# Squares, sums and a reciprocal rearranged for the last two row blocks of a fused matmul and RMS norm

## The chip, the cores and the metric

The kernel runs on one core of a Trainium2 chip. The metric is the time of one execution on the device in microseconds (us); the time before is the median of three runs. One further execution was profiled: the profile's span goes from its first instruction to its last, and its own time is a little longer.

Engine names: PE is the matrix engine (TensorE), DVE is VectorE, ACT is ScalarE, POOL is GpSimd, SP is SyncE, which here only issues transfers. Each engine works through its own queue in order, so an instruction that waits holds up everything queued behind it on that engine.

## The reference

```python
def setup_inputs():
    m, k, n = 2048, 2048, 2048
    # a: m x k, b: k x n, gamma: n, all float32; eps = 1e-5

def reference(a, b, gamma, eps):
    x = np.matmul(a, b)
    rms = np.sqrt(np.mean(x ** 2, axis=-1, keepdims=True) + eps)
    return (gamma * x / rms).astype(np.float32)
```

A row of the output can be scaled only when all 2048 elements of that row of the product are known, since the root takes the mean over the whole row.

## The kernel before

The product's 2048 rows are 16 row blocks of 128, and its 2048 columns are four chunks of 512. A chunk of a row block, 128x512 in fp32, fills one bank of the accumulator memory (PSUM). The first four row blocks are worked as plain products. After that the kernel works on groups: group g holds row blocks 2g and 2g+1, and half j of a group holds two chunks of columns, so that a half is a 2x2 block of chunks. Each half is made by a scheme of seven products in place of eight (Strassen's, in Winograd's form): products 1 to 7 multiply quarters of A or sums of them by quarters of B or differences of them, and sums of the results give the four chunks x11 and x12 (upper row block, first and second chunk) and x21 and x22 (lower row block). `do(n, m)` issues product m of half n: eight matmuls at line 367 that add up into one bank, with the copies between banks that the scheme needs (lines 635 to 641). Some products are worked by the same scheme once more for two halves or groups together (`step` at line 406, `step_seven` at line 448).

The change lies in `last_group` (lines 859 to 985), the last group: g is 7, its row blocks are ra = 14 and rb = 15, and its halves are n and n+1. The code keeps the chunks of both halves in pairs, so x11[0] and x12[0] are row block 14's chunks 0 and 1, x11[1] and x12[1] its chunks 2 and 3, and x21 and x22 are the same for row block 15. TensorE's order at the end is product 6 of half n+1, products 5 of both halves, products 3 of both, products 4 of both. The chunks get complete as follows:

- x11[0] and x11[1] are complete before the last products; they lie in row block 14's output tiles, `xa` (columns 0 to 1023) and `x_tile(ra, 1)`.
- b3[0] and b3[1] are the banks that hold x22's products first. `nc.scalar.copy` at lines 935 and 940 takes them out when products 5 are done, and the sum with x21 gives x22[0] and x22[1], row block 15's chunks 1 and 3. Products 3 are then added on into the same banks, which makes them row block 14's chunks 1 and 3 (x12).
- b2[0] and b2[1] become row block 15's chunks 0 and 2 with products 4, the last of all.

For each row block the squares are made on ScalarE by `square_of` (line 275): one activation that squares its source, writes the squares to a scratch tile and leaves the sum over the row in a column of `msq`. Column 0 of `msq` holds the term with eps. `root` (line 293, the activation at 295) takes the square root of the last sum plus a bias `part`, which VectorE has added up from the earlier columns; `inverse` (line 298, instruction at 300) is VectorE's reciprocal.

What sets the order here is the order of the calls: the schedule is written by hand (`tc.manual_schedule()`), each engine gets its instructions in the order in which the code issues them, and the waits between engines follow from what they read and write. Two engines that read the same bank are also put in order.

After row block 14's reciprocal r_a, its four chunks are scaled by three engines: `by_r` (line 873, ScalarE) scales `left`, `by_r_pool` (line 876, GpSimd) scales `mid` and x11[1], all three already multiplied by gamma, and `scaled_gamma` (line 869, VectorE) multiplies b3[1] by both at once. SyncE's queue issues the transfers to the output in the order of the code (lines 960, 962 and 965). Row block 15 follows in the same manner (lines 971 to 985); its chunks 1 and 3, multiplied by gamma, stand in `wide`, and lines 982 and 985 issue its two transfers.

Of the kernel before, what the change touches and what calls it, by code (L numbers as in the profile page):

```python
# [8 lines left out]
FP32 = mybir.dt.float32  # L9
# [4 lines left out]
ALU = mybir.AluOpType  # L14
# [3 lines left out]
def kernel(  # L18
# [13 lines left out]
    nc = tc.nc  # L32
    P = 128
# [6 lines left out]
    CH = 512  # L40
# [62 lines left out]
    def add(out, in0, in1, op=ALU.add):  # L103
        nc.vector.tensor_tensor(out=out, in0=in0, in1=in1, op=op)  # L104
# [107 lines left out]
    msq = {}  # L212
# [62 lines left out]
    def square_of(mb, src):  # L275
        c = n_sq[mb]
        n_sq[mb] += 1
        sq = sq_pool.tile([P, 2 * CH], BF16, name="sq")
        nc.scalar.activation(out=sq[:, 0:src.shape[-1]], in_=src, func=ACTF.Square,  # L279
                             scale=inv_sqrt_n, accum_out=msq[mb][:, c:c + 1])  # L280

    def square_half(mb, h):
        square_of(mb, x_tile(mb, h))
# [9 lines left out]
    def root(last, part):  # L293
        rms = stat_pool.tile([P, 1], FP32, name="rms")
        nc.scalar.activation(out=rms, in_=last, func=ACTF.Sqrt, bias=part, scale=1.0)
        return rms
# [16 lines left out]
    def finish(mb, order=(0, 1)):  # L313
        if mb not in inverse_of:
            inverse_of[mb] = inverse(rms_of.pop(mb))
        for h in order:
            x = x_half.pop((mb, h))
            nc.vector.scalar_tensor_tensor(  # L318
                out=x, in0=x, scalar=inverse_of[mb], in1=gamma_sb[:, h * HALF:(h + 1) * HALF],
                op0=ALU.mult, op1=ALU.mult)  # L320
            nc.sync.dma_start(out=rows(mb, h * HALF, (h + 1) * HALF), in_=x)
# [302 lines left out]
    def do(n, m, copies=True):  # L624

        if n >= len(halves) or n < 0:
            return
        g, j = halves[n]
        b1, b2, b3 = B1[n % 2], B2[n % 2], B3[n % 2]
        if g >= G2:  # L630
            b1 = b2
        product(g, j, m, {1: b1, 2: b1, 3: b3, 4: b2, 5: b3, 6: b2, 7: B7}[m],
                start=m in (1, 7))
        if m == 1 and g >= G2:
            nc.scalar.copy(out=chunks(n)[0], in_=b2)
        elif m == 1:
            nc.scalar.copy(out=b2, in_=b1)
        elif m == 6:
            nc.scalar.copy(out=b3, in_=b2)  # L639
        elif m == 7 and copies:  # L640
            nc.scalar.copy(out=chunks(n)[2], in_=B7)

    def take(n, what, engine="A"):

        x11, x12, x21, x22 = chunks(n)
        if what == 11:
            copy_on(engine)(out=x11, in_=B1[n % 2])
        elif what == 12:
            copy_on(engine)(out=x12, in_=B3[n % 2])
        elif what == 22:  # L650
            add(x22, B3[n % 2], x21)
        else:
            add(x21, B2[n % 2], x21)
# [205 lines left out]
    def last_group():  # L859
        n = len(halves) - 2  # L860
        g = NG - 1
        ra, rb = 2 * g, 2 * g + 1
        x11, x12, x21, x22 = zip(chunks(n), chunks(n + 1))
        xa, xb = x_tile(ra, 0), x_tile(rb, 0)
        gam = [gamma_sb[:, c * CH:(c + 1) * CH] for c in range(NCH)]
        gam_left = gamma_sb[:, 0:HALF]

        def scaled_gamma(x, src, r, gamma_of_x):
            nc.vector.scalar_tensor_tensor(out=x, in0=src, scalar=r, in1=gamma_of_x,
                                           op0=ALU.mult, op1=ALU.mult)  # L870

        def by_r(x, r):
            nc.scalar.activation(out=x, in_=x, func=ACTF.Copy, scale=r)  # L873

        def by_r_pool(x, r):
            nc.gpsimd.tensor_scalar(out=x, in0=x, scalar1=r, scalar2=1.0,  # L876
                                    op0=ALU.mult, op1=ALU.mult)

        b2, b3 = [B2[(n + j) % 2] for j in range(2)], [B3[(n + j) % 2] for j in range(2)]
        x00, x01 = first_sums(n)[0:2]  # L880
        before = [chunks(n - 2), chunks(n - 1)]


        step_seven(1, B7)
        nc.scalar.copy(out=W2, in_=B7)
        do(n, 6)
        step_seven(6, B7)
        nc.scalar.copy(out=Y2, in_=B7)
        step_seven(2, W2)
        for c in (2, 3):  # L890
            add(before[0][c], W2, before[0][c])
        step_seven(5, Y2)
        nc.scalar.copy(out=x21[1], in_=Y2)
        step_seven(7, X2)
        nc.scalar.copy(out=x21[0], in_=X2)
        square_half(rb - 2, 0)
        add(x21[1], X2, x21[1])
        step_seven(3, Y2)
        for c in (2, 3):
            add(before[1][c], Y2, before[1][c])  # L900
        take_pre(rb - 2)
        square_right(rb - 2)
        do(n - 1, 3)
        take(n - 1, 12)
        step_seven(4, B7)
        add(x21[0], B7, x21[0])
        add(b2[0], b2[0], x21[0])
        finish(rb - 2)


        step(g - 1, 1, X2)
        nc.scalar.copy(out=W2, in_=X2)
        do(n + 1, 1)
        step(g - 1, 6, X2)
        nc.scalar.copy(out=Y2, in_=X2)
        step(g - 1, 2, W2)
        add(x00, W2, x00)
        step(g - 1, 5, Y2)
        add(x11[1], Y2, x11[1])
        square_half(ra - 2, 0)  # L920
        step(g - 1, 7, B7)
        add(x11[0], B7, x11[0])
        add(x11[1], B7, x11[1])
        step(g - 1, 3, Y2)
        add(x01, Y2, x01)
        take_pre(ra - 2)
        square_right(ra - 2)
        step(g - 1, 4, X2)
        add(x11[0], X2, x11[0])
        a_sums(g, (4,))  # L930
        do(n + 1, 6)
        add(b2[1], b2[1], x21[1])
        finish(ra - 2)
        do(n, 5)
        nc.scalar.copy(out=x22[0], in_=b3[0])
        square_of(ra, x11[1])
        add(x22[0], x21[0], x22[0])
        add(x11[1], x11[1], gam[2], ALU.mult)
        do(n + 1, 5)
        nc.scalar.copy(out=x22[1], in_=b3[1])  # L940
        square_of(rb, x22[0])
        wide = a_pool.tile([P, K], FP32, name="a32")
        chunk = [wide[:, c * CH:(c + 1) * CH] for c in range(NCH)]
        add(chunk[1], x22[0], gam[1], ALU.mult)
        add(x22[1], x21[1], x22[1])
        do(n, 3)
        take(n, 12)
        square_half(ra, 0)
        pre_a = stat_pool.tile([P, 1], FP32, name="pre")
        nc.vector.tensor_scalar(out=pre_a, in0=msq[ra][:, 0:1], scalar1=msq[ra][:, 1:2],  # L950
                                scalar2=msq[ra][:, 2:3], op0=ALU.add, op1=ALU.add)
        add(xa, xa, gam_left, ALU.mult)
        do(n + 1, 3)
        square_of(ra, b3[1])
        rms_a = root(msq[ra][:, 3:4], pre_a)
        add(chunk[3], x22[1], gam[3], ALU.mult)
        r_a = inverse(rms_a)
        left, mid = xa[:, 0:CH], xa[:, CH:]
        by_r(left, r_a)
        nc.sync.dma_start(out=rows(ra, 0, CH), in_=left)  # L960
        by_r_pool(mid, r_a)
        nc.sync.dma_start(out=rows(ra, CH, HALF), in_=mid)
        by_r_pool(x11[1], r_a)
        scaled_gamma(x12[1], b3[1], r_a, gam[3])
        nc.sync.dma_start(out=rows(ra, HALF, N), in_=x_tile(ra, 1))
        square_of(rb, x22[1])
        pre_b = stat_pool.tile([P, 1], FP32, name="part")
        nc.vector.tensor_scalar(out=pre_b, in0=msq[rb][:, 0:1], scalar1=msq[rb][:, 1:2],
                                scalar2=msq[rb][:, 2:3], op0=ALU.add, op1=ALU.add)
        do(n, 4)  # L970
        square_of(rb, b2[0])
        add(xb[:, 0:CH], b2[0], gam[0], ALU.mult)
        part = stat_pool.tile([P, 1], FP32, name="part")
        add(part, pre_b, msq[rb][:, 3:4])
        do(n + 1, 4)
        last_sq = stat_pool.tile([P, 1], FP32, name="last_sq")
        sq = sq_pool.tile([P, 2 * CH], BF16, name="sq")
        nc.scalar.activation(out=sq[:, 0:CH], in_=b2[1], func=ACTF.Square, scale=inv_sqrt_n,
                             accum_out=last_sq)
        r_b = inverse(root(last_sq, part))  # L980
        nc.vector.tensor_scalar_mul(out=xb[:, 0:CH], in0=xb[:, 0:CH], scalar1=r_b)
        nc.sync.dma_start(out=rows(rb, 0, CH), in_=xb[:, 0:CH])
        by_r(wide.rearrange("p (c n) -> p c n", n=CH)[:, 1::2, :], r_b)
        scaled_gamma(chunk[2], b2[1], r_b, gam[2])
        nc.sync.dma_start(out=rows(rb, CH, N), in_=wide[:, CH:])
# [40 lines left out]
```

## Time and profile before

| | us |
|---|---|
| median of 3 runs | 219.46 (219.31 to 219.65) |
| the profiled execution's own time | 219.09 |
| its span | 217.3 |
| PE busy in the span | 207.2 (95%) |
| DVE busy | 168.9 (78%) |
| ACT busy | 114.8 (53%) |
| POOL busy | 35.6 (16%) |
| last transfer issued (start of the issue, from the span's start) | 212.88 |

The busy share is a mean over the whole span, so it tells nothing of the last ten microseconds, where the matrix engine runs out of work before the others do. For those the timeline is read: one line for each instruction with its start, its duration, the engine, the line of the code, the operation, and what it writes and reads by the names of the tiles. Row block 14's output tiles appear there as `x`, row block 15's as `x` (columns 0 to 1023) and, before they are copied to the tile named `a`, in a reused buffer named `t_left`; banks appear as `acc`. An instruction with an accumulator output has a second line, the reading of the accumulator.

### The profile page before, as it was taken

How to read it: one execution, taken by the hardware profiler on the slowest of the kernel's cores; microseconds unless marked ns; L12 is line 12 of the kernel's file. 1: busy time of each engine (PE TensorE's matmuls, PEld its weight loads, DVE VectorE, ACT ScalarE, POOL GpSimd, SP SyncE). 2: the span in 40 equal slices, each digit the busy share in tenths (PEclk: the TensorE clock that was granted, in tenths of full speed). 3: DMA queues.
4: the chain of work that ended last, by engine and by line, in shares of the span. 5: the costliest groups of instructions: out<-in, count | busy, mean ns of one | idle time of the engine just before them, and what ended most of it. 6: DMA issues, size and time to landing. Idle time of an engine off the chain costs nothing.

```text
span 217.3 us, 2979 instructions
## 1 busy us (share of the span) xinstructions
PE 207.2 (95%) x1016; PEld 96.2 (44%) x1016; DVE 168.9 (78%) x333; ACT 114.8 (53%) x225; POOL 35.6 (16%) x74
## 2 busy tenths in 40 slices
PE   7999999999999999999999999999999999999950
PEld 3444544444455444444444444444444444444420
DVE  1128869999899987888975899399759899688871
ACT  2110002900599569598626952594776834654761
POOL 7554444334001000100021001102010000000020
PEclk9999999999999999999999999999999999999996
DMA  7999999999959688988675975599996872040446
GB/s 155 173 202 210 200 206 208 213 208 216 403 192 383 285 233 234 302 354 244 157 239 176 337 244 91 193 238 265 263 317 161 267 133 82 14 186 10 193 134 252
DMA packets 37039, 46.60 MB, mean 214 GB/s; under 512 B 22560, under 2 KB 26656, under 8 KB 35744
## 3 DMA queue, kind: packets, MB, share of 16 engines
q0 software_dynamic: 10608, 23.86, 45.0%
q1 hardware_dynamic: 26144, 22.29, 34.1%
q10 hardware_dynamic: 272, 0.26, 0.3%
q8 instruction: 8, 0.13, 0.2%
q14 instruction: 7, 0.06, 0.1%
HBM read 34.60 MB, written 16.78 MB: 236 GB/s over the span
## 4 chain that ended last, share of the span: by engine, by line
PE 87%; DVE 4%; DMA 3%; ACT 2%; issue 1%; POOL 1%; ACTq 0%; POOLq 0%
PE acc L367 58%; PE acc L457 16%; DMA early<-in_a_dram 3%; PE acc L406 3%; PE acc L448 2%; PE tbank L406 2%; PE tbank L486 2%; PE tbank L188 2%; ACT sq L279 1%; DVE x L318 1%; DVE x L104 1%; ACT a L873 1%; POOL b L118 0%; PE acc L201 0%; PE tbank L201 0%
## 5 line engine op out<-in xcount | busy, mean ns | idle before, releaser
L457 PE MATMUL acc<-b,head_at 128*128 128x512 bf16 x176 | 43.0, 379 | 0.3 <-DMA b<-in_b_dram 0.3
L367 PEld LDWEIGHTS <-s 128*128 128x128 f16 (+1 forms) x280 | 27.4, 98 | 33.1 <-DVE s L344 0.3
L279 ACT ACTIVATE sq<-x 128x1024 bf16<-128x1024 f32 (+1 forms) x31 | 31.9, 1030 | 18.9 <-DVE x L104 14.3
L318 DVE SCALAR_TENSOR_TENSOR x<-x,r,gamma_sb 128x1024 f32<-128x1024 f32 x28 | 35.0, 1282 | 0.5
L367 PE MATMUL acc<-b,head_at 128*128 128x512 bf16 x136 | 33.8, 379 | 0.0
L104 DVE TENSOR_TENSOR x<-acc,x 128x512 f32<-128x512 f32 x34 | 22.7, 687 | 9.8 <-PE acc L406 4.2
L367 PEld LDWEIGHTS <-head_at 128*128 128x128 f16 (+1 forms) x192 | 18.7, 98 | 22.2
L367 PE MATMUL acc<-b,at_even 128*128 128x512 bf16 x112 | 26.1, 379 | 0.0
L457 PEld LDWEIGHTS <-head_at 128*128 128x128 bf16 x176 | 16.9, 98 | 19.6 <-issue 0.6
L230 ACT ACTIVATE sq<-a 128x1024 bf16<-128x1024 f32 x22 | 23.3, 1058 | 2.2 <-DMA a<-in_a_dram 1.7
L367 PE MATMUL acc<-b,s 128*128 128x512 bf16 x104 | 24.4, 379 | 0.0
L367 PEld LDWEIGHTS <-at_even 128*128 128x128 f16 x160 | 15.6, 98 | 18.6
L367 PE MATMUL acc<-early,s 128*128 128x512 bf16 x96 | 23.7, 379 | 0.0
L118 POOL DMA_DIRECT2D b<-in_b_dram x32 | 17.2, 540 | 20.5 <-DMA b<-in_b_dram 14.1
L367 PE MATMUL acc<-t_left,s 128*128 128x512 bf16 x80 | 18.9, 379 | 0.0
L496 ACT COPY x<-acc 128x512 f32<-128x512 f32 x7 | 4.0, 581 | 25.3 <-PE acc L457 25.3
L193 DVE COPY head_at<-tbank 128x1024 bf16<-128x1024 bf16 x7 | 4.8, 692 | 7.7 <-PE tbank L188 7.7
L639 ACT COPY acc<-acc 128x512 f32<-128x512 f32 x12 | 6.9, 574 | 7.4 <-PE acc L367 7.3
L104 DVE TENSOR_TENSOR x<-tbank,x 128x512 f32<-128x512 f32 x9 | 6.2, 691 | 4.2 <-PE tbank L486 4.1
L876 POOL TENSOR_SCALAR x<-x,r 128x512 f32<-128x512 f32 x2 | 1.4, 685 | 48.8 <-DVE r L300 48.8
L149 POOL CAST pace<-at_even 128x1 f32<-128x1 f16 x3 | 1.7, 551 | 37.5 <-DMA at_even<-a 37.5
L367 PE MATMUL acc<-early,head_at 128*128 128x512 bf16 x32 | 7.7, 379 | 0.0
(155 smaller groups left out, 259.6 us busy)
## 6 DMA issues: line engine op xcount, KB each, us to landing
out_dram<-x SPq DMA_DIRECT2D x29, 512.0 KB, 3.0
a<-in_a_dram POOLq DMA_DIRECT2D x9, 1024.0 KB, 6.3
b<-in_b_dram POOLq DMA_DIRECT2D x32, 256.0 KB, 9.9
a<-in_a_dram POOLq DMA_DIRECT2D x4, 512.0 KB, 9.8
early<-in_a_dram POOLq DMA_DIRECT2D x7, 256.0 KB, 10.0
gamma_sb<-in_gamma_dram POOLq DMA_DIRECT2D x2, 512.0 KB, 9.9
head_at<-in_a_dram POOLq DMA_DIRECT2D x1, 1024.0 KB, 9.4
out_dram<-x SPq DMA_DIRECT2D x3, 256.0 KB, 2.6
```

Source lines behind the costliest of these rows:

```text
L104: nc.vector.tensor_tensor(out=out, in0=in0, in1=in1, op=op)
L118: nc.gpsimd.dma_start(out=raw[j][kp][:, t, :], in_=b[lo:lo + P, j * HALF:(j + 1) * HALF])
L188: nc.tensor.matmul(view[:, t, r, :], ah(kp)[:, r, t * P:(t + 1) * P], identity, is_transpose=True, start=(t == 0 and r == 0), stop=(t == 1 ...
L193: nc.vector.tensor_copy(out=head_at[:, 2 * kp:2 * kp + 2, :, :], in_=view)
L230: nc.scalar.activation(out=junk, in_=a32[mb][:, h * HALF:(h + 1) * HALF], func=ACTF.Square, scale=2.0 ** -8, accum_out=n2[:, h:h + 1])
L279: nc.scalar.activation(out=sq[:, 0:src.shape[-1]], in_=src, func=ACTF.Square, scale=inv_sqrt_n, accum_out=msq[mb][:, c:c + 1])
L318: nc.vector.scalar_tensor_tensor(out=x, in0=x, scalar=inverse_of[mb], in1=gamma_sb[:, h * HALF:(h + 1) * HALF], op0=ALU.mult, op1=ALU.mult)
L367: nc.tensor.matmul(bank, lhsT[:, kp, :], rhs, start=(start and kp == 0), stop=(kp == KP - 1), skip_group_check=not start)
L406: nc.tensor.matmul(bank, lhsT[:, k, :], rhs, start=(m in (1, 7) and k == 0), stop=(k == KQ - 1), skip_group_check=m not in (1, 7))
L448: nc.tensor.matmul(bank, lhsT[:, k, :], rhs[:, k, :], start=(m in (1, 7) and k == 0), stop=(k == KQ - 1), skip_group_check=m not in (1, 7))
L457: nc.tensor.matmul(bank, head_at[:, kt, r, :], head_rhs(c, kt), start=(kt == 0), stop=(kt == KT - 1))
L639: nc.scalar.copy(out=b3, in_=b2)
```

## The change

Only the order and the grouping of the work in `last_group` change. Row block 14's chunk x11[0] is squared by itself ahead of line 935's copy. Its chunk 1 is no longer copied out of b3[0] into `xa` and squared there together with chunk 0 in one 1024-wide activation; it is squared out of the bank, and the multiply with gamma reads the bank and writes `mid`, while `left` is multiplied by itself. Row block 14 now has four sums of squares beside column 0 of `msq`, and the bias of its root is added up in two steps, `pre` and `pre_a`. The sum x22[1] moves ahead of the products 3, and its square moves from behind row block 14's scaling to the place behind b3[0]'s square, with the sum `pre_b` ahead of row block 14's reciprocal. The multiplies of x11[1] and of x22[0] with gamma move behind the two multiplies of row block 14's left half, and the multiply of x22[1] with gamma (`chunk[3]`) moves from the place ahead of the reciprocal `r_a` to the place behind row block 14's scaling.

TensorE's, GpSimd's and SyncE's instructions and their order stay the same. VectorE has two instructions more.

```diff
         add(b2[1], b2[1], x21[1])
+        square_of(ra, x11[0])
         finish(ra - 2)
         do(n, 5)
         nc.scalar.copy(out=x22[0], in_=b3[0])
         square_of(ra, x11[1])
         add(x22[0], x21[0], x22[0])
-        add(x11[1], x11[1], gam[2], ALU.mult)
         do(n + 1, 5)
         nc.scalar.copy(out=x22[1], in_=b3[1])
         square_of(rb, x22[0])
+        add(x22[1], x21[1], x22[1])
+        pre = stat_pool.tile([P, 1], FP32, name="pre")
+        nc.vector.tensor_scalar(out=pre, in0=msq[ra][:, 0:1], scalar1=msq[ra][:, 1:2],
+                                scalar2=msq[ra][:, 2:3], op0=ALU.add, op1=ALU.add)
+        do(n, 3)
+        square_of(ra, b3[0])
+        square_of(rb, x22[1])
+        left, mid = xa[:, 0:CH], xa[:, CH:]
+        add(mid, b3[0], gam[1], ALU.mult)
+        add(left, left, gam[0], ALU.mult)
+        add(x11[1], x11[1], gam[2], ALU.mult)
+        pre_a = stat_pool.tile([P, 1], FP32, name="pre")
+        add(pre_a, pre, msq[ra][:, 3:4])
+        do(n + 1, 3)
+        square_of(ra, b3[1])
+        rms_a = root(msq[ra][:, 4:5], pre_a)
         wide = a_pool.tile([P, K], FP32, name="a32")
         chunk = [wide[:, c * CH:(c + 1) * CH] for c in range(NCH)]
         add(chunk[1], x22[0], gam[1], ALU.mult)
-        add(x22[1], x21[1], x22[1])
-        do(n, 3)
-        take(n, 12)
-        square_half(ra, 0)
-        pre_a = stat_pool.tile([P, 1], FP32, name="pre")
-        nc.vector.tensor_scalar(out=pre_a, in0=msq[ra][:, 0:1], scalar1=msq[ra][:, 1:2],
-                                scalar2=msq[ra][:, 2:3], op0=ALU.add, op1=ALU.add)
-        add(xa, xa, gam_left, ALU.mult)
-        do(n + 1, 3)
-        square_of(ra, b3[1])
-        rms_a = root(msq[ra][:, 3:4], pre_a)
-        add(chunk[3], x22[1], gam[3], ALU.mult)
+        pre_b = stat_pool.tile([P, 1], FP32, name="part")
+        nc.vector.tensor_scalar(out=pre_b, in0=msq[rb][:, 0:1], scalar1=msq[rb][:, 1:2],
+                                scalar2=msq[rb][:, 2:3], op0=ALU.add, op1=ALU.add)
         r_a = inverse(rms_a)
-        left, mid = xa[:, 0:CH], xa[:, CH:]
         by_r(left, r_a)
         nc.sync.dma_start(out=rows(ra, 0, CH), in_=left)
         by_r_pool(mid, r_a)
         nc.sync.dma_start(out=rows(ra, CH, HALF), in_=mid)
         by_r_pool(x11[1], r_a)
         scaled_gamma(x12[1], b3[1], r_a, gam[3])
         nc.sync.dma_start(out=rows(ra, HALF, N), in_=x_tile(ra, 1))
-        square_of(rb, x22[1])
-        pre_b = stat_pool.tile([P, 1], FP32, name="part")
-        nc.vector.tensor_scalar(out=pre_b, in0=msq[rb][:, 0:1], scalar1=msq[rb][:, 1:2],
-                                scalar2=msq[rb][:, 2:3], op0=ALU.add, op1=ALU.add)
+        add(chunk[3], x22[1], gam[3], ALU.mult)
         do(n, 4)
```

## The prediction

> **What bounds the kernel now.** I read the page's chain first.
>
> ```profile
> PE 87%; DVE 4%; DMA 3%; ACT 2%; issue 1%; POOL 1%; ACTq 0%; POOLq 0%
> ```
>
> TensorE sets the end nearly everywhere, but the diff leaves TensorE's instructions and their order as they are, so the change can only act where TensorE no longer decides: the end. Next the timeline of the last 14 us, all engines (start, duration, engine, line, operation, and in brackets the idle time before it).
>
> ```profile
> 204.29 0.57 ACT L649 COPY x<-acc 128x512 f32<-128x512 f32 x1
> 205.79 1.89 PE L367 MATMUL acc<-t_left,head_at 128*128 128x512 bf16 x8
> 206.79 0.29 ACT L295 ACTIVATE rms<-msq,pre 128x1 f32<-128x1 f32 x1
> 207.40 0.68 DVE L104 TENSOR_TENSOR a<-t_left,gamma_sb 128x512 f32<-128x512 f32 x1
> 207.52 1.89 PE L367 MATMUL acc<-early,head_at 128*128 128x512 bf16 x8
> 208.00 0.16 DVE L300 RECIPROCAL r<-rms 128x1 f32<-128x1 f32 x1
> 208.19 0.72 ACT L873 ACTIVATE x<-x,r 128x512 f32<-128x512 f32 x1 [1.10 <-DVE r L300]
> 208.26 1.36 POOL L876 TENSOR_SCALAR x<-x,r 128x512 f32<-128x512 f32 x2 [48.84 <-DVE r L300]
> 208.82 0.61 ACT L279 ACTIVATE sq<-t_left 128x512 bf16<-128x512 f32 x1
> 209.55 0.60 ACT L279 ACTIVATE sq<-acc 128x512 bf16<-128x512 f32 x1
> 209.85 0.39 SPq L965 DMA_DIRECT2D out_dram<-x  x1
> 210.27 0.60 ACT L978 ACTIVATE sq<-acc 128x512 bf16<-128x512 f32 x1
> 210.28 0.69 DVE L104 TENSOR_TENSOR x<-acc,gamma_sb 128x512 f32<-128x512 f32 x1 [0.44 <-ACT sq L279]
> 211.13 0.29 ACT L295 ACTIVATE rms<-last_sq,part 128x1 f32<-128x1 f32 x1 [0.17 <-DVE part L104]
> 212.88 0.33 SPq L985 DMA_DIRECT2D out_dram<-a  x1
> ```
>
> Row 14's root was ready at 207.08 (206.79 + 0.29), yet its reciprocal ran at 208.00, behind the product of 207.40 on VectorE. TensorE's last product ended at 209.41 (207.52 + 1.89), yet its square (L978) began at 210.27: ScalarE was still scaling row 14 and squaring two other chunks, one of them from t_left (x22[1]), which had long been there. So 0.86 us of row 15's chain is ScalarE's queue. Then the transfers, in stretches of 0.25 us; the last two numbers are the DMA engines' busy share and GB/s.
>
> ```profile
> 212.25:212.50 0.25, 0.00 (x0) 0.00 (x0) 0.25 (x1) 0.25 (x1) 0.00 (x0) 1.00 1.00 410
> 212.50:212.75 0.25, 0.00 (x0) 0.00 (x0) 0.25 (x1) 0.25 (x1) 0.00 (x0) 1.00 0.53 213
> 212.75:213.00 0.25, 0.00 (x0) 0.00 (x0) 0.05 (x1) 0.10 (x1) 0.00 (x0) 1.00 0.10 33
> 213.00:213.25 0.25, 0.00 (x0) 0.00 (x0) 0.00 (x0) 0.00 (x0) 0.00 (x0) 1.00 0.90 344
> ```
>
> From 209.75 to 215.7 the DMA engines are busy with the two rows (2.1 MB at about 400 GB/s where undisturbed); only here, between row 14's last bytes and row 15's first, do they idle. Against 400 GB/s that is 0.12 + 0.23 + 0.04 = 0.38 us. So the end has two limits close together: row 15's arithmetic and the queue of bytes.
>
> **The parts, with their costs.** *Square of x11[0] added ahead of L935's copy (ScalarE).* It costs 0.63 us plus its accumulator read, 0.73 in all (from 203.66 to 204.39 for such a square of SBUF). ScalarE idles 1.16 us there, from 199.66 to 200.81, so it ends near 200.41: nothing. Without that cover L935's copy would move by up to 0.73, and TensorE, which adds to that bank from 202.34 while the copy ends at 201.40, would still not wait.
>
> *L649's copy replaced by a square out of PSUM, the 1024-wide square dropped, x22[1]'s square put here.* The square of b3[0] starts at 204.42 (after the accumulator read that ends at 204.39), is done with its read 0.69 later at 205.11; x22[1]'s follows to 205.87. The next one, of b3[1], can start when TensorE is done at 205.96; before it started at 206.07. Gain under 0.1, and not used (below). x22[1]'s sum, moved ahead on VectorE to 203.48, finds L940's copy done at 203.13: no wait, and its place is counted next.
>
> *VectorE up to the reciprocal.* Its adds of 128x512 start 0.61 apart (203.48, 204.09, 204.69). The product `mid` reads the bank that ScalarE squares and waits for it: by the row of 210.28, which started 0.04 behind such a square's read, at 205.15. Queued behind it: left, x11[1], pre_a, chunk[1], pre_b, the reciprocal; the root waits for pre_a. Their starts: 205.15 + 0.60 + 0.61 + 0.61 = 206.97 pre_a; + 0.07 (as between 197.30 and 197.37) chunk[1]; + 0.61 pre_b; + 0.19 (206.07 to 206.26) the reciprocal, at 207.84. The root, with pre_a at 207.12, ends near 207.5, so it doesn't decide. The reciprocal thus gains 0.16, not the 0.9 that its move suggests: the split product, the two new sums and the wait for the bank fill the place of the product moved behind it. Bounds: if the wait cost nothing it would come 0.6 earlier (bound by the root, at about 207.5, 0.5 of gain); if the new small sums each drained the engine for their whole length, about 0.25 later. I take 0.16.
>
> *Row 15's chain.* Scaling row 14 starts at 208.03; the square of b2[0] now follows at once, 208.66 to 209.35 with its read; the last square starts at TensorE's end, 209.44 (0.83 gained), its sum ready at 210.13. VectorE: L869's multiply at 208.03, chunk[3] 0.67 later at 208.70, b2[0]'s product behind the square of that bank at 209.39, part at 209.99 to 210.14, root 0.10 later at 210.24 against 211.13. So 0.89 is gained up to the root, and with it the issues of both last transfers (212.17 and 212.88), if nothing stands in chunk[3]'s way.
>
> *Something does: GpSimd.* chunk[3] reads two SBUF tiles while GpSimd scales x11[1]; before, VectorE idled there. The trace shows such meetings where GpSimd copies 128x1:
>
> ```profile
> 109.88 0.71 POOL L149 CAST pace<-at_even 128x1 f32<-128x1 f16 x1 [20.86 <-DMA at_even<-a]
> 158.34 0.18 POOL L149 CAST pace<-at_even 128x1 f32<-128x1 f16 x1 [7.96 <-DMA at_even<-a]
> 109.85 0.69 DVE L344 TENSOR_TENSOR at_even<-at_even 128x1024 f16<-128x1024 f16 x1
> ```
>
> With VectorE idle it took 0.18, beside a two-tile VectorE instruction 0.71, until that ended. Bounds: nothing; or VectorE waits for one GpSimd instruction, 0.68 (half of 1.36); or GpSimd waits for one VectorE instruction, 0.65. I take the last, since it is what the casts show: GpSimd's first scaling ends at 208.78 (208.26 - 0.16 + 0.68), chunk[3], waiting since 208.70, runs to 209.4, and GpSimd's second scaling from there to 210.1 (209.62 before), so that row 14's last issue (209.85) comes at 210.3. The Trainium skill (SBUF — State Buffer, section "SBUF: two separate sides") says that one port pair is shared, that a VectorE instruction with two SBUF inputs and a GpSimd one that reads SBUF exclude each other, and that the first holds it for the whole instruction; the casts agree (0.71 against 0.18). By it the first to start decides, so the sum would be mine or the rival's in which GpSimd goes first.
>
> *The bytes.* From issue to first bytes takes about 0.8 (208.94 to 209.75, 212.17 to 213.0). Row 14's first 512 KB flow from 209.6 to about 210.95; its last 512 KB, issued at 210.3, are ready at 211.1, as late as before when they stood behind the others. So row 14 ends where it did. Row 15's first bytes are ready at 212.1 and its others at 212.8, before row 14 is out: the idle 0.38 is filled, and the 0.89 of the chain is cut to that. Not all engines end together; I take 0.30 of it, bounds 0.1 to 0.38. **Sum:** the profiled execution, 219.09 (span 217.3 and 1.8 around it), becomes 218.79; the median of the runs is 0.37 above it, so 219.46 becomes 219.16.
>
> **Rivals.** *No meeting:* chunk[3] and GpSimd don't hold one another. Row 14 is then out 0.16 earlier and the gap filled as well: 0.46, 219.00. For it: GpSimd's first scaling ran at 0.68 beside a VectorE multiply, though that one read PSUM. Against: the casts.
>
> *GpSimd goes first:* chunk[3] waits to 209.46, b2[0]'s product starts at 210.07, the root at 210.92, 0.2 earlier than before; the bytes follow: 0.2, 219.26. For it: GpSimd's two scalings stood without a gap between them (1.36 for both). Against: in the casts it was GpSimd that waited.
>
> *The bytes aren't the limit:* row 14's transfers ran slower (287 and 262 GB/s in two of the stretches from 211.25 to 211.75), and if row 15's issue alone decides, up to 0.89 is gained: 218.57. Against: the volume and 400 GB/s.
>
> *Slower:* transfers that overlap disturb each other. When the third transfer came up behind two others near 210.7, the next four stretches gave 311, 426, 287 and 262 GB/s, mean 322. After the change row 15's transfers come up behind row 14's from 212.1 on, with 1.27 MB to go (225 KB of row 14 by the stretches from 212.1, and 1.05 MB). At 322 GB/s that takes 3.95 us and ends at 216.05 instead of 215.7: 0.35 slower, 219.81. It decides below 1.27 MB / 3.6 us = 353 GB/s. Against: two full-width transfers behind one another kept 408 GB/s between 203 and 205.
>
> **Chances.** Forecast 0.40, no meeting 0.20, GpSimd first 0.13, bytes not the limit 0.12, slower 0.15. A change under 0.2% (0.44 us) is what a measurement of this kernel can hardly tell from none: faster means under 219.02, slower over 219.90. Faster: all of the bytes rival (0.12), somewhat over half of the no-meeting one, which lies on the bound (0.12), and the part of the forecast in which the wait for the bank costs less than taken (0.12): 0.36. Slower by that much: a good half of the slow rival, whose rate may fall further: 0.09. Within: 0.55. The forecast's own range is 218.90 (the reciprocal earlier by half of its bound) to 219.36 (a gap filled by 0.1 alone). The range reaches from the near end of the bytes rival to the near part of the slow one: 218.68 to 219.65.
>
> **What would show it.** In the changed profile the reciprocal of row 14 stands near 207.84 and its neighbours on VectorE without idle time behind 205.15; the last square starts behind TensorE, near 209.44; chunk[3] or GpSimd's second scaling is longer than 0.69; the last root stands near 210.2; the DMA engines show no gap near 212.75 and end about 0.3 earlier. It is wrong if TensorE's last product starts later than 207.52, if the reciprocal is no earlier than 208.00, or if the bytes still pause and the time falls by the whole 0.89.

## The result

| | before | changed |
|---|---|---|
| median of 22 runs each, us | 219.39 | 218.89 |
| the profiled execution's own time, us | 219.09 | 218.90 |
| its span, us | 217.3 | 217.1 |

The ratio is 0.9974 with a 95% interval of 0.9963 to 0.9985: the change makes the kernel 0.15% to 0.37% faster, 0.50 us by the medians (0.30 was forecast; the 219.46 that the forecast started from was the median of the first three of these 22 runs). 218.89 is inside the predicted range, 0.27 below the forecast's 219.16. By the medians the gain is a little past the bound of 0.2%, so the case that had the chance of 0.36 came true and not the one of 0.55; the interval reaches to both sides of that bound.

Here are the lines of the changed kernel's timeline on which the readings rest, with the same columns as before.

```profile
205.38 0.69 DVE L104 TENSOR_TENSOR x<-acc,gamma_sb 128x512 f32<-128x512 f32 x1 [0.78 <-ACT sq L279]
205.99 1.28 DVE L104 TENSOR_TENSOR x<-x,gamma_sb 128x512 f32<-128x512 f32 x2
207.19 0.15 DVE L104 TENSOR_TENSOR pre<-pre,msq 128x1 f32<-128x1 f32 x1
207.26 0.68 DVE L104 TENSOR_TENSOR a<-x,gamma_sb 128x512 f32<-128x512 f32 x1
207.44 0.30 ACT L295 ACTIVATE rms<-msq,pre 128x1 f32<-128x1 f32 x1 [0.45 <-DVE pre L104]
207.77 1.89 PE L367 MATMUL acc<-early,head_at 128*128 128x512 bf16 x8
207.86 0.26 DVE L962 TENSOR_SCALAR part<-msq 128x1 f32<-128x1 f32 x1
208.05 0.15 DVE L300 RECIPROCAL r<-rms 128x1 f32<-128x1 f32 x1
208.30 1.84 POOL L876 TENSOR_SCALAR x<-x,r 128x512 f32<-128x512 f32 x2 [48.92 <-DVE r L300]
208.90 0.68 DVE L104 TENSOR_TENSOR a<-t_left,gamma_sb 128x512 f32<-128x512 f32 x1
209.41 0.38 SPq L968 DMA_DIRECT2D out_dram<-x  x1
209.75 0.60 ACT L981 ACTIVATE sq<-acc 128x512 bf16<-128x512 f32 x1 [0.23 <-PE acc L367]
210.17 0.33 SPq L971 DMA_DIRECT2D out_dram<-x  x1
210.47 0.29 ACT L295 ACTIVATE rms<-last_sq,part 128x1 f32<-128x1 f32 x1
211.51 0.33 SPq L985 DMA_DIRECT2D out_dram<-x  x1
212.22 0.33 SPq L988 DMA_DIRECT2D out_dram<-a  x1
```

Two issues of the kernel before, row 14's second and the first of row 15's:

```profile
209.36 0.38 SPq L962 DMA_DIRECT2D out_dram<-x  x1
212.17 0.33 SPq L982 DMA_DIRECT2D out_dram<-x  x1
```

TensorE's last product starts at 207.77 here and at 207.52 before. It was late before the first changed instruction ran: TensorE's two products 5 already start at 199.13 against 198.89, and in the profiles of the runs below the last product's start lies anywhere from 207.56 to 209.01. From the start of the products 5 to that of the last product it is 8.63 or 8.64 us in every one of these profiles, so the difference arises further up, where nothing was changed. So from here on every time is counted from the start of TensorE's last product in the same profile, which I call zero. Against it, the last square has moved from 2.75 to 1.98, right behind TensorE's end at 1.89 (the idle time in front of it now ends with TensorE), and the issues of row 15's transfers from 4.65 and 5.36 to 3.74 and 4.45: 0.91 earlier. Yet the time fell by only about half of that. The stretches of the DMA engines in the changed kernel (the last two numbers are their busy share and GB/s) show where the rest went.

```profile
212.25:212.50 0.25, 0.00 (x0) 0.00 (x0) 0.00 (x0) 0.00 (x0) 0.00 (x0) 0.50 1.00 410
212.50:212.75 0.25, 0.00 (x0) 0.00 (x0) 0.00 (x0) 0.00 (x0) 0.00 (x0) 0.50 0.99 393
212.75:213.00 0.25, 0.00 (x0) 0.00 (x0) 0.00 (x0) 0.00 (x0) 0.00 (x0) 0.50 0.93 361
213.00:213.25 0.25, 0.00 (x0) 0.00 (x0) 0.00 (x0) 0.00 (x0) 0.00 (x0) 0.50 1.17 459
```

The pause between the two rows' bytes, 213 and 33 GB/s before, is gone. Row 15's bytes now follow row 14's without a break, and what the chain gained beyond that is spent in the queue; the runs without a part of row 14's bytes test this.

### The profile page after: what moved, and what is told of

It reads as the page before. It is cut to its first block, busy times and chain, and to the rows that moved or that the text cites. A ratio compares the mean times of both kernels' runs of the same rounds, so it can differ in the third digit from the quotient of the medians.

```text
span 217.1 us, 2964 instructions
## 1 busy us (share of the span) xinstructions
PE 206.8 (95%) x996; PEld 97.0 (45%) x1016; DVE 168.9 (78%) x335; ACT 114.5 (53%) x226; POOL 35.9 (17%) x74
## 4 chain that ended last, share of the span: by engine, by line
PE 95%; ACT 1%; issue 1%; DVE 1%; ACTq 0%
PE acc L367 63%; PE acc L457 17%; PE acc L406 3%; PE acc L448 2%; PE tbank L406 2%; PE acc L167 2%; PE tbank L486 2%; PE tbank L188 2%; ACT a L873 1%; PE acc L201 0%; PE tbank L201 0%; PE acc L178 0%; PE tbank L178 0%; DVE head_at L193 0%; ACT sq L981 0%
## 5 line engine op out<-in xcount | busy, mean ns | idle before, releaser
L457 PE MATMUL acc<-b,head_at 128*128 128x512 bf16 x171 | 42.1, 379 | 0.2
L367 PE MATMUL acc<-b,head_at 128*128 128x512 bf16 x134 | 33.7, 379 | 0.3
L367 PE MATMUL acc<-t_left,s 128*128 128x512 bf16 x77 | 18.4, 379 | 0.1
```

What stands on the lines that cost most here:

```text
L367: nc.tensor.matmul(bank, lhsT[:, kp, :], rhs, start=(start and kp == 0), stop=(kp == KP - 1), skip_group_check=not start)
L457: nc.tensor.matmul(bank, head_at[:, kt, r, :], head_rhs(c, kt), start=(kt == 0), stop=(kt == KT - 1))
```

## The experiments

All times in this table are from the traces, counted from zero as above. "Reciprocal" and "root" are row 14's reciprocal and row 15's root; "row 14 out" is when the first and the last of the 16 DMA engines wrote its last completion for row 14, "row 15 in" the first packet of row 15, "end" the last completion of all. These last three are read from the single packets in the traces, in which each transfer has 16 completions, one from each DMA engine. The medians stand beside the median of the kernel before on the same chip.

| kernel | reciprocal | root | row 14 out | row 15 in | end | median us (before) | ratio, 95% interval |
|---|---|---|---|---|---|---|---|
| before | 0.48 | 3.61 | 4.96 to 5.42 | 5.48 | 8.34 | | |
| changed | 0.28 | 2.70 | 4.72 to 5.24 | 4.73 | 7.89 | 218.89 (219.39) | 0.9974, 0.9963 to 0.9985 |
| square_only | 0.48 | 2.85 | 4.95 to 5.40 | 4.95 | 8.05 | 218.93 (219.25) | 0.9993, 0.9981 to 1.0005 |
| chunk3_only | -0.12 | 3.00 | 4.32 to 4.80 | 4.87 | 7.74 | 218.62 (219.25) | 0.9972, 0.9961 to 0.9984 |
| chunk3_late | 0.28 | 2.70 | 4.77 to 5.21 | 4.77 | 7.85 | 218.97 (219.25) | 0.9996, 0.9981 to 1.0011 |
| mid_last | -0.42 | 2.71 | 4.08 to 4.52 | 4.58 | 7.44 | 218.35 (219.25) | 0.9959, 0.9947 to 0.9972 |
| before_less_bytes | 0.48 | 3.61 | 3.60 to 3.96 | 5.48 | 8.34 | 219.41 (219.36) | 1.0008, 0.9992 to 1.0024 |
| after_less_bytes | 0.29 | 2.71 | 3.41 to 3.79 | 4.58 | 7.45 | 218.43 (219.36) | 0.9957, 0.9943 to 0.9971 |
| mid_last_less_bytes | -0.41 | 2.71 | 2.72 to 3.09 | 4.59 | 7.45 | 218.64 (219.36) | 0.9969, 0.9954 to 0.9985 |
| after_again | 0.29 | 2.71 | 4.71 to 5.23 | 4.72 | 7.87 | 218.87 (219.36) | 0.9982, 0.9968 to 0.9997 |
| after_beside | 0.29 | 2.71 | 4.76 to 5.23 | 4.77 | 7.86 | 218.92 (219.39) | 0.9981, 0.9963 to 0.9999 |
| mid_last_beside | -0.42 | 2.71 | 4.07 to 4.52 | 4.58 | 7.44 | 218.15 (219.39) | 0.9944, 0.9927 to 0.9962 |

The intervals of the timed ratios are some 0.3 us wide to either side, as wide as the effects; the differences between the kernels are read from the column "end", which repeats within 0.03 (7.89, 7.87 and 7.86 for three profiles of the changed kernel, 7.44 twice for mid_last). The other kernels have one profile each. A ratio is not that of the two medians beside it and can differ from it by 0.001 (chunk3_late: 0.9996, by the medians 0.9987).

**square_only: x22[1]'s square alone.**

```diff
         rms_a = root(msq[ra][:, 3:4], pre_a)
+        square_of(rb, x22[1])
         add(chunk[3], x22[1], gam[3], ALU.mult)
 ...
         nc.sync.dma_start(out=rows(ra, HALF, N), in_=x_tile(ra, 1))
-        square_of(rb, x22[1])
```

> The kernel before with one line moved: x22[1]'s square from behind row 14's scaling to ahead of it, into the 1.10 us in which ScalarE waits for the reciprocal, and nothing else. My theory (bytes): row 14's reciprocal and first bytes stay (0.48 and 2.25 from the start of TensorE's last product), the last root comes about 0.7 to 0.8 earlier, but only the gap of 0.38 between the rows' bytes can be filled: 0.25 to 0.38 gained, about 219.1. Rival (row 15's issues alone set the end): the whole 0.7 to 0.8, about 218.7.

```profile
207.65 1.89 PE L367 MATMUL acc<-early,head_at 128*128 128x512 bf16 x8
208.13 0.15 DVE L300 RECIPROCAL r<-rms 128x1 f32<-128x1 f32 x1
210.50 0.29 ACT L295 ACTIVATE rms<-last_sq,part 128x1 f32<-128x1 f32 x1 [0.16 <-DVE part L104]
```

The reciprocal stayed at 0.48, the root came 0.76 earlier (3.61 to 2.85), and the end 0.29 earlier. Row 15's first packet came when the first engine was through with row 14 (both 4.95). So 0.47 of the chain's gain was lost in the queue of bytes. The timed ratio alone doesn't tell the two theories apart (its interval holds no gain as well as 0.4 us); the trace does.

**chunk3_only: the reciprocal's move alone.**

```diff
         rms_a = root(msq[ra][:, 3:4], pre_a)
-        add(chunk[3], x22[1], gam[3], ALU.mult)
         r_a = inverse(rms_a)
 ...
         nc.sync.dma_start(out=rows(ra, HALF, N), in_=x_tile(ra, 1))
+        add(chunk[3], x22[1], gam[3], ALU.mult)
         square_of(rb, x22[1])
```

> The kernel before with one line moved: chunk[3]'s product from ahead of row 14's reciprocal to behind row 14's scaling, and nothing else. My theory (bytes): the reciprocal comes as soon as the root and the 1024-wide product allow, about 0.6 earlier (0.48 to -0.1 from the start of TensorE's last product), ScalarE's queue behind it moves along, the last root comes about 0.6 to 0.7 earlier, so bytes and chain both gain: 0.5 to 0.7, about 218.8. Rival (the gain came from x22[1]'s square being out of ScalarE's way, and the reciprocal matters little): under 0.2, about 219.3.

```profile
207.66 0.15 DVE L300 RECIPROCAL r<-rms 128x1 f32<-128x1 f32 x1
207.78 1.89 PE L367 MATMUL acc<-early,head_at 128*128 128x512 bf16 x8
210.78 0.29 ACT L295 ACTIVATE rms<-last_sq,part 128x1 f32<-128x1 f32 x1 [0.17 <-DVE part L104]
211.82 0.33 SPq L982 DMA_DIRECT2D out_dram<-x  x1
```

One line moved in the kernel before brings the reciprocal 0.60 earlier and, in the trace, the end 0.60 earlier, more than the whole change's 0.45 (the timed ratios, 0.9972 and 0.9974, do not tell the two apart). Row 14 is out at 4.80, before row 15's first packet at 4.87, which is its issue (4.04) plus 0.83: the bytes came early enough for the whole gain of the chain, 0.61 at the root, to count. Here the reciprocal gets its whole gain because nothing was put in front of it; in the changed kernel it got 0.20.

**mid_last: the wait for the bank taken out of the reciprocal's way.**

```diff
-        add(mid, b3[0], gam[1], ALU.mult)
         add(left, left, gam[0], ALU.mult)
         add(x11[1], x11[1], gam[2], ALU.mult)
+        add(mid, b3[0], gam[1], ALU.mult)
```

> The changed kernel with its product mid (which reads the bank b3[0] and waits for that bank's square) moved behind the products left and x11[1] on VectorE. Times counted from the start of TensorE's last product. My theory (the output bytes of both row blocks set the end, so it follows row 14's reciprocal): the 0.78 us wait in front of mid goes, row 14's reciprocal falls from 0.28 to about -0.4, the first bytes from 2.04 to about 1.35, the last root stays at 2.70, and yet the end comes 0.4 to 0.5 earlier than in the changed kernel, near 218.4 against 218.9. Rival (the end follows row 15's issues alone, and the 0.91 gained on them was lost elsewhere): the reciprocal moves as well, but the root and both last issues stay, and so does the time, 218.9.

VectorE's timeline in this run:

```profile
204.68 0.27 DVE L944 TENSOR_SCALAR pre<-msq 128x1 f32<-128x1 f32 x1
204.86 1.28 DVE L104 TENSOR_TENSOR x<-x,gamma_sb 128x512 f32<-128x512 f32 x2
206.06 0.68 DVE L104 TENSOR_TENSOR x<-acc,gamma_sb 128x512 f32<-128x512 f32 x1
207.69 0.17 DVE L300 RECIPROCAL r<-rms 128x1 f32<-128x1 f32 x1
```

The 0.78 us of idle time in front of `mid` is gone: the two products that read no bank fill it, and the reciprocal stands 0.42 before the start of TensorE's last product instead of 0.28 behind it. The root did not move (2.70, 2.71) and the end came 0.45 earlier than in the changed kernel. The rival, by which only row 15's issues count, would have left the time where it was. And now there is a pause between the rows again; stretches of this run:

```profile
212.11:212.36 0.25, 0.00 (x0) 0.00 (x0) 0.25 (x1) 0.25 (x1) 0.00 (x0) 0.97 0.73 295
212.36:212.61 0.25, 0.00 (x0) 0.00 (x0) 0.13 (x1) 0.18 (x1) 0.00 (x0) 0.50 0.26 98
212.61:212.86 0.25, 0.00 (x0) 0.00 (x0) 0.00 (x0) 0.00 (x0) 0.00 (x0) 0.50 0.60 229
```

With row 14 out at 4.08 to 4.52 and row 15 in at 4.58, its issue (3.75) plus 0.83, the bytes have stopped being the limit.

**chunk3_late: no meeting of VectorE and GpSimd.**

```diff
-        add(chunk[3], x22[1], gam[3], ALU.mult)
         do(n, 4)
 ...
         add(part, pre_b, msq[rb][:, 3:4])
+        add(chunk[3], x22[1], gam[3], ALU.mult)
```

> The changed kernel with chunk[3]'s product moved behind the sum part, so that VectorE reads no two SBUF tiles while GpSimd scales x11[1]. My theory: GpSimd's second scaling falls from 1.16 to 0.69 us, row 14's last issue comes about 0.2 earlier, but its bytes stand behind the first 512 KB in any case: no gain from that; chunk[3] now ends just behind the last root and costs row 15's chain up to 0.1: within 0.1 us of the changed kernel's 218.9. Rival (the meeting of VectorE and GpSimd costs the end its 0.47): 218.4 to 218.6.

The line of GpSimd's two scalings (shortest, mean and longest duration in ns, then the starts), in the changed kernel:

```profile
L876 POOL TENSOR_SCALAR x<-x,r x2: 689/923/1157, 208.3 to 209.0; 128x512 f32<-128x512 f32 x2
```

and in chunk3_late:

```profile
L876 POOL TENSOR_SCALAR x<-x,r x2: 681/684/687, 208.8 to 209.5; 128x512 f32<-128x512 f32 x2
```

So the meeting is real and costs GpSimd 0.47 us: VectorE's chunk[3] keeps its 0.68, and GpSimd's second scaling, which starts 0.09 later, stretches from 689 to 1157 ns. That is the order of the casts, and in kind it agrees with the exclusion that the Trainium skill states (SBUF — State Buffer, section "SBUF: two separate sides"); its length is taken up in the last section. But taking it away moved row 14's last issue by 0.27 (2.40 to 2.13) and the end by 0.04: the meeting costs the kernel nothing that these runs can tell.

**Leaving out 512 KB.** In three kernels the transfer of row block 14's right half is left out (of the kernel before, the changed one and mid_last), and with it these 512 KB of the output:

```diff
-        nc.sync.dma_start(out=rows(ra, HALF, N), in_=x_tile(ra, 1))
```

> The kernel before without the transfer of row block 14's right half (its 512 KB are left out of the output). My theory: before the change row 15's bytes waited for their issue, not for row 14's bytes, so the end stays at 8.34 from the start of TensorE's last product, at most 0.1 earlier. Rival (row 14's bytes cost the end here too, by a slower row 15): 0.3 or more earlier.

> The changed kernel without the transfer of row block 14's right half (its 512 KB are left out of the output); all arithmetic stays. Times from the start of TensorE's last product. My theory (row 14's bytes stand ahead of row 15's): row 15's first bytes come 0.83 after their issue, at about 4.57 instead of 4.73, with no engine left behind, and the last transfer ends near 7.45 instead of 7.89: 0.4 gained. Rival (the end follows row 15's issues alone): 7.89, no gain.

> The kernel of the run mid_last without the transfer of row block 14's right half (its 512 KB are left out of the output). My theory: with row 14's reciprocal 0.7 earlier its bytes are out (4.08 to 4.52) before row 15's can start (4.58), so the end is now set by row 15's chain: 7.44 as in mid_last, within 0.1. Rival (bytes still set the end): 0.3 or more earlier.

The kernel before ends at 8.34 with those bytes and without; the changed kernel at 7.89 with them and at 7.45 without; mid_last at 7.44 and 7.45. So row 14's bytes set the end in the changed kernel, and in neither of the other two. In the changed kernel they cost 0.44, the difference between the 0.89 by which its end would have fallen and the 0.45 by which it fell.

**Repeats, side by side.**

> The changed kernel itself, unedited, beside the others on one chip: 0.45 to 0.55 below the kernel before, and the same steps as in its first profile: reciprocal 0.28, last root 2.70, last transfer out at 7.89 from the start of TensorE's last product, each within 0.05.

> The changed kernel, unedited, beside mid_last_beside on one chip: 0.45 to 0.5 below the kernel before, ratio 0.9977 to 0.998.

> The kernel of the run mid_last, unedited, beside the changed kernel on one chip. My theory: 0.45 below the changed kernel and 0.9 below the kernel before, by the last transfer's end in the profiles (7.44 against 7.89 and 8.34 from the start of TensorE's last product). Rival (the first reading of 218.35 was favoured by the chip): no more than 0.2 below the changed kernel.

All steps of the changed kernel came out as in its first profile. mid_last was 0.77 below it by the medians on one chip (218.15 and 218.92), more than the 0.45 of the traces; the rest is not explained (in its first run, on another chip, it was 0.90 below the kernel before, as the traces give). The rival, by which no more than 0.2 would be left, is out. The interval of mid_last's ratio, 0.9927 to 0.9962, is 0.8 to 1.6 us below the kernel before, that of the changed kernel beside it 0.9963 to 0.9999. It is the fastest version of this study.

## Why the prediction came out as it did

*The two limits.* Right. The chain to row 15's issues gained 0.91 (0.89 said), and the end fell by 0.45 in the trace, because the bytes of the two rows stand in one queue. The rival by which the bytes aren't the limit would have had the whole 0.89. The runs without 512 KB show it directly.

*ScalarE's first parts.* Right, they moved nothing by more than 0.02: the copy out of b3[0] starts 1.93 behind the start of the products 5 (1.92 before), and the square of b3[1] at -1.47 (-1.45 before).

*The reciprocal.* Right. It gained 0.20 (0.16 said), not the 0.60 that the move brings alone in chunk3_only, nor the 0.9 up to the root. `mid` waits 0.78 us for the square that reads its bank, and the products and sums queued behind it took the spacings that I read from the profile of before. The root ahead of it waits 0.45 for pre_a, as said, without deciding. That the wait is what kept the reciprocal back is shown by mid_last, where it comes 0.70 earlier.

*The last square.* Right: 1.98 against the forecast 1.92 (209.44 less 207.52), waiting for TensorE. Of the 0.91, chunk3_only and square_only get 0.61 and 0.76 of their own; the two overlap.

*The meeting on GpSimd.* Right in kind: VectorE first, GpSimd's second scaling longer by 0.47 (0.65 was the bound, and 0.62 went into the sum, 208.78 to 209.4). The step that failed is what I made of it: "so that row 14's last issue (209.85) comes at 210.3", and "So row 14 ends where it did". The issue came 0.07 later than before (2.33 to 2.40) and not 0.45, for two reasons in the rows. GpSimd started 0.2 earlier and lost 0.47, so it ended only 0.27 later, where I had 0.48 (209.62 to 210.1). And I let the issue come 0.2 behind GpSimd's end, about as before (209.62 to 209.85); but there it stood behind the issue of 209.36, 0.49 from start to start (0.49 and 0.48 in chunk3_late and square_only, where GpSimd is likewise done 0.2 earlier), while in the changed kernel it comes 0.03 behind GpSimd's end. With 0.83 to the first bytes it was ready at 3.23, ahead of the first completion of row 14's first 512 KB at 3.39 (211.16 less 207.77). So row 14 did end earlier, by 0.18 at its last engine (5.42 to 5.24).

*The sum.* The filled pause was taken as 0.30; by itself, in square_only, it brought 0.29, and in the changed kernel 0.27 is left for it (0.45 less 0.18, a subtraction and not a measurement). The missing term is the 0.18. With it the sum is near that of my rival without a meeting (0.46), though the meeting takes place: its number was right and its reason wrong. That not all engines end together, for which I had taken 0.30 of the 0.38, the packets show: on the mean of the 16 engines row 14 was out 0.20 earlier (5.19 to 4.99) and row 15 0.61 (8.20 to 7.59), about the whole pause of 0.38 and the 0.20 together. But the engines now end from 7.28 to 7.89, before from 8.11 to 8.34, and the last of them, which sets the time, gained 0.45. The median fell by 0.50.

*The signs.* One that I had named for being wrong did appear: TensorE's last product starts later than 207.52. It does not count against the account, since the 0.25 were there before the first changed instruction, and one and the same program varies by nearly as much (207.56 to 207.77 in three profiles of the changed kernel).

*The slow rival.* From 212.50 to 215.00 in the changed kernel the ten stretches of 0.25 us average 409 GB/s, above the 353 from which it would have decided: row 15's transfers, coming up behind row 14's, were not slowed. Row 14's own slow stretches are still there (320 and 246 GB/s in the two stretches from 211.25 to 211.75); their cause was not tried.

```profile
211.25:211.50 0.25, 0.00 (x0) 0.00 (x0) 0.25 (x2) 0.25 (x1) 0.00 (x0) 1.00 1.48 320
211.50:211.75 0.25, 0.00 (x0) 0.00 (x0) 0.25 (x1) 0.25 (x1) 0.00 (x0) 1.00 0.90 246
```

## What to carry to other kernels

When work on the last results is shortened, ask what their transfers queue behind: here half of what the chain gained was lost to the bytes of the row block ahead, and it was that row's start, not the last row's, that was worth the next step. When an instruction is moved off a queue, look at what is moved onto it at the same time, a wait for a shared bank above all, and put instructions that need nothing in front of the one that waits: one line moved behind two others gained as much again as the whole change. Count times from a common event of each profile when the runs differ further up by more than the effect.

## What the runs showed of the hardware that was not expected

The meeting of VectorE and GpSimd is one-sided here: VectorE's product of two SBUF tiles took 0.68 as always, and only GpSimd's row grew, by 0.47, in all eight profiles in which the two meet (1157 to 1159 ns). By the rows the exclusion is not exact. chunk[3] started at 208.90, 0.09 before GpSimd's first scaling ended, without growing, and GpSimd's second scaling lost 0.47 of the 0.59 that were then left of chunk[3]'s row (the cast of 109.88 lost 0.53 of 0.66). Nor do the starts of the rows tell which of the two goes first: in the kernel before, a cast that takes 0.18 when alone took 0.76 beside a VectorE instruction on two SBUF tiles that started behind it.

```profile
149.15 0.76 POOL L149 CAST pace<-at_even 128x1 f32<-128x1 f16 x1 [8.69 <-DMA at_even<-a]
149.19 0.68 DVE L344 TENSOR_TENSOR s<-head_at,s 128x1024 f16<-128x1024 f16 x1
```

The time from the start of an issue on SyncE to the first packet, where nothing stood ahead of it, was 0.82 to 0.83 in every one of these profiles (1.21 to 2.04, 3.75 to 4.58). A transfer queued behind another sets in as the engines get through with the one ahead, without a pause: row 14's first three engines are through at 4.72, 4.77 and 4.80 in the changed kernel, and row 15's first three packets start at 4.73, 4.77 and 4.80 (the packets do not name their engine, so the match is by time), while the last of the engines is through half a microsecond later (5.24).
